# Where the gelu of the dense experts lives: an SBUF tile or the matmul's own PSUM bank

## The chip, the cores and the metric

One core of one Trainium2 chip runs the kernel. The metric is the device time of one execution in microseconds, the median of several runs. The engines are PE (TensorE matmul; PEld its weight loads), DVE (VectorE), ACT (ScalarE), POOL (GpSimd) and SP (SyncE, which here only issues DMAs). Each works through a queue of its own in order; semaphores tie the queues together.

## The reference, cut to what matters

One step of a one-layer hybrid decoder for 1024 prompt tokens and 32 sample rows: adaptive norm, input projection, dilated attention and a delta-rule mixer side by side, output projection, second norm, and a layer of product-key experts. The change touches only the last:

```python
eid  = jnp.take_along_axis(cid, pos, axis=-1)        # 8 heads x 16 experts of 16384 for every token
gate = jax.nn.softmax(top_s, axis=-1)
act  = jax.nn.gelu(jnp.einsum('nd,nhkd->nhk', hb, expert_u[eid]), approximate=False)
return jnp.einsum('nhk,nhkd->nd', gate * act, expert_v[eid])
```

Every expert is one unit: a row of `expert_u` (1024 values) makes a dot with the token, its gelu is multiplied with the gate, and the product scales a row of `expert_v`.

## The kernel before, in words

The kernel computes the experts in two ways at once. Tiles 5, 6 and 7 of the prompt and the sample rows gather the chosen rows by indirect DMA (issued on POOL) and work on DVE: `row<-row,gh` is the product with the token and its sum, `gh<-row,co,gh` or `ga<-row,co,ga` adds a scaled row of `expert_v` to a sum held in PSUM. Tiles 0 to 4 (640 tokens, `n`) are computed densely by `dense` (line 1615): all 16384 units for every token, with a gate of zero where an expert was not chosen.

In `dense`, 128 blocks `b` of 128 units are taken in 32 groups of four (`NG`). `hidden(b)` loads the block's part of `expert_u`, transposed, in two pieces `u`, and splits each into two float32r parts: `uh` by an ACT cast, `ul` by a subtraction on POOL (`split2`, line 1611). For each half `h` of the tokens (320 columns) PE adds 24 matmuls (8 blocks of channels times three products of parts, `mm3`) into one bank of the PSUM tag `d`, which has four banks (`open_psum(ctx, "densep", d=4)`). Then ACT takes the gelu out of the bank into an SBUF tile `act` (two buffers), DVE multiplies it in place with the gates `g`, ACT casts the product to `ch`, and DVE subtracts to get `cl` (`split`, line 230). `values` loads and splits rows of `expert_v` into `vh` and `vl` (POOL, for some blocks DVE). `output` adds 12 matmuls of `ch`, `cl` against `vh`, `vl` into a bank of the same four, and DVE adds the bank to `dacc` in SBUF. A group is thus eight hidden half-tiles and ten output tiles on PE, all of them taking banks of the tag `d`.

The streams are put side by side by `weave`, with a rough meter of engine time, from `run(weave((routed(p_at, [6, 7, NT], "right"), True), fill=[some, all_experts]))` on: the routing of the gathered tiles, the gathers and the dense experts share all queues, and the rest of the dense work runs beside the remaining gathers to the end. The order in each engine's queue is then set by a planner that runs a timeline with costs of its own while the program is built (`schedule_with_timeline_sim=True`); it also adds the semaphore waits, and a bank is given to the next tile once the last instruction that reads it is done. Every instruction is recorded under line 196, the helper that passes calls on, so the trace is read by tiles.

Of the kernel before, what the change touches and what calls it, by code (L numbers as in the profile page):

```python
# [64 lines left out]
def _shape_constants():  # L65
# [20 lines left out]
    # relative bias along distance, from 1023 down  # L86
# [7 lines left out]
    # the sample rows' keys: 4 of every 16 far rows, the near ones, the new ones  # L94
# [35 lines left out]
class _Meter:  # L130
    """a rough count of the engines' time, by which streams of work are put side by side."""
# [43 lines left out]
class _Ring(dict):  # L175
    """tiles by number, made when first asked for."""
# [25 lines left out]
def tile_hybrid_step(ctx, tc, ins, outs):  # L202
# [9 lines left out]
    def open_psum(es, name, side="left", **tags):  # L212
        """banks of PSUM by tag; returns what gives the next one of a tag."""
        pool = es.enter_context(tc.tile_pool(name=name, bufs=1, space=bass.MemoryType.PSUM, side=side, reuse_waits="tile"))

        def bank(tag, n=512):
            return pool.tile([128, n], FT, tag=tag, name=tag, bufs=tags[tag])

        return bank
# [10 lines left out]
    def split(src, hi, lo, eng=None):  # L230
        """src as a sum of two float32r parts."""
        sc.copy(hi, src)
        (eng or ve).tensor_tensor(lo, src, hi.bitcast(FT), op=OP.subtract)

    def piece(pool, src, kn, eng, bufs, wbufs):
        """1024 columns of weights, of kn blocks of rows: as two float32r parts."""
        w = pool.tile([128, 1024], FT, tag="w", name="w", bufs=wbufs).rearrange("p (k c) -> p k c", k=kn)
        sy.dma_start(w, src)
        hl = [pool.tile([128, 1024], FR, tag=f"w{x}", name=f"w{x}", bufs=bufs).rearrange("p (k c) -> p k c", k=kn) for x in "hl"]
        split(w, *hl, eng=eng)  # L240
        return hl

    def mm3(out, l, r, first, last):
        """a product of split operands, to float32's accuracy; or of unsplit ones."""
        if len(l) == 1:
            te.matmul(out, l[0], r[0], start=first, stop=last)
            return
        te.matmul(out, l[0], r[0], start=first, stop=False)
        te.matmul(out, l[0], r[1], start=False, stop=False)
        te.matmul(out, l[1], r[0], start=False, stop=last)  # L250
# [3 lines left out]
    def rsqrt(pool, x, scale, bias, shape, name, floor=None):  # L254
        """1 / sqrt(scale * x + bias), with one Newton step behind the table."""
        n = shape[0]
        t = [pool.tile([128] + list(shape[1:]), FT, tag=f"{name}{j}", name=f"{name}{j}", bufs=2)[:n] for j in range(3)]
        v, y, z = t
        if floor is None:
            ve.tensor_scalar(v, x, scale, bias, op0=OP.mult, op1=OP.add)  # L260
        else:
            ve.tensor_scalar(v, x, floor, None, op0=OP.max)
        sc.activation(y, v, AF.Sqrt)
        ve.reciprocal(y, y)
        ve.tensor_tensor(z, y, y, op=OP.mult)
        ve.scalar_tensor_tensor(z, v, -0.5, z, op0=OP.mult, op1=OP.mult)
        ve.scalar_tensor_tensor(y, z, 1.5, y, op0=OP.add, op1=OP.mult)
        return y
# [7 lines left out]
    def weave(*streams, fill=(), ahead=AHEAD):  # L276
        """several streams side by side: (steps, whether a step waits for the one before). The one that is ready
        first by the meter goes on; fill: streams that only go along."""
# [34 lines left out]
    def open_picked(es, name, tiles, ring=None):  # L313
        """the chosen experts of some tiles, and their gates."""
# [12 lines left out]
    def mod_rows(pool, seg, i, tag, n, bufs=1):  # L327
        """one of the six modulation vectors, a row for every token of tile i."""
# [16 lines left out]
    # ---------------------------------------------------------------- modulation, first norm  # L345
# [7 lines left out]
    def ada_rows(pa, pp, scT, r, bufs):  # L353
# [17 lines left out]
        if r == 2:  # L371
            # the second norm's weights times its scale
            n2 = pa.tile([128, 512], FT, tag="adab", name="n2", bufs=2)
            for g in range(2):
                sy.dma_start(n2[32 * g:32 * g + 32, :], _ap(A["norm2_g"], 512 * g, [[0, 32], [1, 512]]))
            ve.scalar_tensor_tensor(md[:64], md[:64], 1.0, n2[:64], op0=OP.add, op1=OP.mult)
# [17 lines left out]
    def scaled(out, pt, k, ab=ab1):  # L394
        """shift and scale of a norm, of the prompt's transposed rows; k: the block of channels."""
        sc.activation(out, pt, AF.Identity, scale=ab[:, 0, k, 0:1], bias=ab[:, 1, k, 0:1])

    def scaled_sample(out, pt, ab):
        """the same of the sample rows."""
# [4 lines left out]
    def norm_rows(pa, tiles):  # L404
        """the rows of some tiles over their root mean square."""
# [16 lines left out]
    def norm_in(pa, pp, tiles, put):  # L422
        """first norm of some tiles, transposed: put(k, part) for the channels 128 k.. ."""
# [22 lines left out]
    # ---------------------------------------------------------------- projections  # L446
    def project(pw, pp, hT, tiles, bufs=3, wbufs=2, rbufs=1, engs=(gp,)):
        """all columns of w_in for some token tiles: (tile, its column)."""
# [74 lines left out]
    # ---------------------------------------------------------------- the delta-rule heads  # L523
# [11 lines left out]
    def delta_consts(rc):  # L535
# [5 lines left out]
        # tiles that keep zeros where a block is empty  # L541
# [16 lines left out]
    def log_decay(pool, pp, lt, c0, n):  # L558
        """token-major logarithm of the decay."""
# [7 lines left out]
    def key_norms(pool, pp, sqk, n, nj):  # L567
        """1 / max(|kk|, 1e-12), token-major."""
# [8 lines left out]
    def spread(pool, pp, rn, p, n, nj):  # L577
        """the norms of a pair of heads over their columns, transposed."""
# [9 lines left out]
    def group_norm(pool, pp, y, n, bv, g, c0):  # L588
        """y token-major; normalised per head, the bonus and the gate put on, into columns c0.. of the mix."""
# [24 lines left out]
    def rwkv_prompt(pp, side, qs):  # L614
        """quarters of the prompt, 256 tokens each, in chunks of 64; heads go in two groups of four, side by side."""
        n = 256
        both = (0, 1)
        for qi in qs:
            t0 = 256 * qi
            with ExitStack() as es:  # L620
# [3 lines left out]
                with ExitStack() as e2:  # L624
                    pt_ = open_pool(e2, "rwt", side)

                    def shifted(c0, k, tag="shx", out=None):
                        """channels c0.., mixed with the token before."""
# [89 lines left out]
                with ExitStack() as e3:  # L718
# [14 lines left out]
                    # inverses of the 32-blocks: two partitions a block, for its even and its odd rows  # L733
# [30 lines left out]
                def chunk(j, gq, ych, py):  # L764
                    """two chunks of 64 tokens, four heads."""
# [41 lines left out]
                    # right-hand sides [A | M_ak V], then (I - M_ab)^-1 of them  # L807
# [88 lines left out]
    # ---------------------------------------------------------------- dilated attention  # L896
    def attn_bias(pa, pp):
        """the queries' scale by head halves; the relative bias along distance, and of the last 128 queries."""
# [29 lines left out]
    def attn_prompt(pp, side, tiles, nb=None, pa=None, wide=False):  # L928
        """some query tiles of the prompt."""
# [102 lines left out]
    def attn_sample(pp, side, pa=None):  # L1032
        """the sample rows: partition = (row, head, position), four rows at a time."""
        with ExitStack() as es:
# [20 lines left out]
            # masked queries: columns (p, b, h, s)  # L1055
# [103 lines left out]
    def rwkv_sample(pp, side):  # L1159
        n = NS  # L1160
        with ExitStack() as es:
# [11 lines left out]
            # every channel mixed with the token before  # L1173
# [53 lines left out]
            # one partition a (row, head, half of the values)  # L1227
# [38 lines left out]
    # ---------------------------------------------------------------- output projection, second norm  # L1266
    def weights(pa, src, bufs=NW):
        """256 columns of weights in pieces of two blocks of rows; src(first block)."""
# [6 lines left out]
    def shared_banks(pp, tiles):  # L1275
        """256 columns of PSUM for every tile, two tiles in a bank; and whether a tile is its bank's first."""
# [3 lines left out]
    def project_out(pa, pp, tiles, new_x1, new_h2, bufs=NW):  # L1280
        """x1 and the second-norm rows of some tiles; new_x1, new_h2: where they go, the latter transposed."""
# [72 lines left out]
    # ---------------------------------------------------------------- product keys  # L1354
    def fold_keys(pa, pp, bufs):
        """the query projection times the sub-keys."""
# [15 lines left out]
    def route_scores(pa, pp, h2, tops, bufs=NW):  # L1372
        """every half key's scores, for the tiles in h2; the sixteen best of each. The sample rows: a quarter of the
        partitions for every fourth head."""
# [32 lines left out]
    def open_tops(es, name, tiles, side="left", ring=None):  # L1407
        """what route_scores leaves for route_pick."""
# [8 lines left out]
    def route_pick(pick, tops, i, eng=ve):  # L1417
        """the sixteen best experts of every head of a tile's tokens, and their softmax."""
# [38 lines left out]
        for h in range(nh + 1):  # L1457
            if h < nh:
                # the candidate whose place is asked for leaves its expert, the others more (those before it by wrapping)
# [15 lines left out]
    # ---------------------------------------------------------------- experts, gathered  # L1475
# [6 lines left out]
    def expert_dots(gat, pg, eid, gate, h2, npick):  # L1482
        """gate * gelu(u . h2), partition = token."""
# [30 lines left out]
    def sum_rows(gat, acc, co, eid, npick):  # L1514
        """acc = sum of co * v, partition = token."""
# [15 lines left out]
    def gather_sample(gat, pg, acc_bank):  # L1531
        """the sample rows, with a quarter of their experts on each quarter of the partitions."""
# [16 lines left out]
    # ---------------------------------------------------------------- experts, all of them  # L1549
# [3 lines left out]
    def spread_gates(pa, pp, i, c0, iota128, stages):  # L1553
        """the gates of a tile's tokens over all experts: g_d[., second key, first key, token]."""
# [28 lines left out]
        for t4 in range(32):  # L1583
            ps = pp("sp")
            sh = [128, 2, 128]
            for x in range(2):
# [5 lines left out]
                for j in range(2):  # L1592
                    t = slice(o + j, o + j + 1)
                    e = SPREAD[2 * x + j]
                    if e == "sc":
                        # gate * max(1 - |key - column|, 0)
# [18 lines left out]
    def dense(pa, pp, acc, h2T, tiles):  # L1615
        """every expert for the tokens of some tiles: products of split operands."""
# [6 lines left out]
        def hidden(b):  # L1623
# [9 lines left out]
            for h in range(2):  # L1633
# [7 lines left out]
                t = pa.tile([128, n // 2], FT, tag="act", name="act", bufs=2)  # L1641
                sc.activation(t, ps[:, :n // 2], AF.Gelu)
# [54 lines left out]
    # ---------------------------------------------------------------- the order of the work  # L1697
# [192 lines left out]
    def routed(pp, tiles, side):  # L1890
        """from the mix to the experts, for some gathered tiles."""
# [107 lines left out]
```

## Time and profile before

| what | value |
|---|---|
| median of 3 runs | 3811.39 us (3810.4 to 3816.43) |
| profiled execution, span | 3802.4 us |
| PE busy | 3473.4 us (91%) |
| DVE busy | 2899.8 us (76%) |
| POOL busy | 2107.3 us (55%) |
| ACT busy | 1428.1 us (38%) |
| mean DMA rate | 258 GB/s |

The page gives the profiled execution's time as its span, from the first to the last instruction; no other time of that execution is shown. Busy time says how long an engine had an instruction in it; matmuls are pipelined, and a busy PE is not PE at its peak. Rows name what is written and what is read, as `act<-act,g`, with buffer numbers left out, and "idle before" or "waits" tell which instruction's end released a waiting one.

### The profile page before, as it was taken

The numbers are of one execution on the slowest core, as the hardware profiler recorded it, in microseconds if no ns is written. First come the engines' busy times: TensorE is split into PE (matmuls) and PEld (weight loads), VectorE is DVE, ScalarE is ACT, GpSimd is POOL, SyncE is SP. The second block draws the span as 40 slices with busy tenths as digits, with TensorE's granted clock in tenths as the row PEclk, the third lists the DMA queues.
The fourth block names the chain that finished last, engine by engine and source line by source line (L and its number), as shares of the span: only waits on it lengthen the run. The fifth ranks groups of instructions, "written<-read, shape, count | busy, mean of one in ns | idle before, by whom it ended". The sixth has DMA issues, their size and how long they took to land.

```text
span 3802.4 us, 57197 instructions
## 1 busy us (share of the span) xinstructions
PE 3473.4 (91%) x19618; PEld 2873.5 (76%) x19618; DVE 2899.8 (76%) x6059; ACT 1428.1 (38%) x3124; POOL 2107.3 (55%) x1842
## 2 busy tenths in 40 slices
PE   7999999789889888969999989999999999999998
PEld 3878678567768664547877879888887878788886
DVE  2655364588688566777878999888888888888898
ACT  5544344336766654542411322222222222222221
POOL 3232021015555356656655777677677767677775
PEclk8999999899999899989999999999999999999999
DMA  9643695553765667749988779999889898899998
GB/s 292 196 143 115 189 280 170 164 181 134 241 210 179 206 222 229 259 156 328 324 303 283 230 263 327 320 317 312 308 303 318 306 315 303 307 312 320 327 324 311
DMA packets 592528, 981.58 MB, mean 258 GB/s; under 512 B 78323, under 2 KB 354620, under 8 KB 589420
## 3 DMA queue, kind: packets, MB, share of 16 engines
q1 hardware_dynamic: 467788, 524.84, 43.1%
q0 software_dynamic: 124448, 453.08, 33.9%
q8 instruction: 155, 2.54, 0.3%
q14 instruction: 137, 1.12, 0.1%
HBM read 882.97 MB, written 94.78 MB: 257 GB/s over the span
## 4 chain that ended last, share of the span: by engine, by line
PE 36%; DVE 23%; DMA 19%; issue 11%; POOL 8%; ACT 3%; SPq 1%; POOLq 0%; DVEq 0%; ACTq 0%
PE at L196 10%; PE d L196 9%; DMA u<-in_uT 8%; PE rw L196 5%; PE pj L196 5%; POOL row L196 4%; PE rs L196 3%; DVE gh L196 3%; DVE act L196 2%; DVE row L196 2%; DVE cl L196 2%; PE sp L196 2%; DMA row<-in_expert_v,eid 2%; POOL vl L196 2%; POOL ul L196 2%
## 5 line engine op out<-in xcount | busy, mean ns | idle before, releaser
L196 PE MATMUL d<-h2T,uh 128*128 128x320 f32 x4096 | 908.1, 311 | 11.6 <-ACT h2T L196 7.0
L196 PEld LDWEIGHTS d<-h2T,uh 128*128 128x128 f32 x4096 | 689.7, 189 | 21.2 <-ACT h2T L196 7.3
L196 PE MATMUL d<-h2T,ul 128*128 128x320 f32 x2048 | 632.8, 310 | 0.3 <-POOL ul L196 0.3
L196 POOL DMA_INDIRECT row<-in_expert_u,eid x416 | 405.7, 975 | 264.3 <-DVE co L196 90.0
L196 PE MATMUL d<-vl,ch 128*128 128x512 f32 x1280 | 512.2, 401 | 43.6 <-POOL vl L196 43.6
L196 PE MATMUL d<-vh,ch 128*128 128x512 f32 x1280 | 486.4, 401 | 51.2 <-DVE dacc L196 26.9
L196 DVE CUSTOM_DVE_ANT_0 row<-row,gh 128x1024 f32<-128x1024 f32 x416 | 499.4, 1210 | 34.7 <-DMA row<-in_expert_u,eid 26.0
L196 POOL DMA_INDIRECT row<-in_expert_v,eid x416 | 406.4, 977 | 183.5 <-DVE gh L196 66.2
L196 PE MATMUL d<-vh,cl 128*128 128x512 f32 x1280 | 505.6, 396 | 0.8 <-DVE cl L196 0.7
L196 POOL TENSOR_SCALAR oha<-c_iota,tr 128x128 f32<-128x128 f32 x320 | 309.6, 974 | 310.8 <-PE sp L196 297.9
L196 POOL TENSOR_TENSOR ul<-u,uh 128x512 fp32r<-128x512 f32 x256 | 336.6, 1324 | 139.7 <-ACT uh L196 129.7
L196 ACT CAST vh<-v 128x512 fp32r<-128x512 f32 x256 | 157.5, 620 | 623.2 <-DMA v<-in_expert_v 447.9
L196 PEld LDWEIGHTS d<-h2T,ul 128*128 128x128 f32 x2048 | 386.2, 189 | 2.7 <-issue 1.6
L196 DVE SCALAR_TENSOR_TENSOR gh<-row,co,gh 128x1024 f32<-128x1024 f32 x285 | 364.9, 1280 | 27.7 <-DMA row<-in_expert_v,eid 26.0
L196 PEld LDWEIGHTS d<-vh,ch 128*128 128x128 f32 x1280 | 243.0, 191 | 129.8 <-DVE dacc L196 43.3
L196 DVE TENSOR_TENSOR act<-act,g 128x320 f32<-128x320 f32 x256 | 279.2, 1090 | 77.2 <-ACT act L196 72.8
L196 POOL TENSOR_TENSOR wl<-w,wh 128x1024 fp32r<-128x1024 f32 x50 | 122.5, 2453 | 388.7 <-ACT wh L196 353.9
L196 PEld LDWEIGHTS d<-vl,ch 128*128 128x128 f32 x1280 | 244.4, 191 | 112.0 <-POOL vl L196 62.1
L196 POOL TENSOR_TENSOR vl<-v,vh 128x512 fp32r<-128x512 f32 x224 | 289.5, 1301 | 34.7 <-ACT vh L196 30.3
L196 ACT CAST ch<-act 128x320 fp32r<-128x320 f32 x256 | 117.7, 460 | 495.4 <-DVE act L196 464.2
L196 PEld LDWEIGHTS d<-vh,cl 128*128 128x128 f32 x1280 | 244.9, 191 | 53.9 <-DVE cl L196 2.0
L196 ACT CAST uh<-u 128x512 fp32r<-128x512 f32 x256 | 154.0, 617 | 257.0 <-DMA u<-in_uT 166.2
(449 smaller groups left out, 6932.7 us busy)
## 6 DMA issues: line engine op xcount, KB each, us to landing
u<-in_uT SPq DMA_DIRECT2D x256, 256.0 KB
v<-in_expert_v SPq DMA_DIRECT2D x256, 256.0 KB
w<-wq_d SPq DMA_DIRECT2D x224, 256.0 KB
g_d<-stage SPq DMA_DIRECT2D x20, 2048.0 KB
g<-g_d SPq DMA_DIRECT2D x64, 640.0 KB
w<-in_w_in SPq DMA_DIRECT2D x75, 512.0 KB
w<-in_w_out SPq DMA_DIRECT2D x112, 256.0 KB
adaw<-in_ada_w SPq DMA_DIRECT2D x32, 512.0 KB
```

Of the source, the lines that this page charges most:

```text
L196: return f(*a, **k)
```

## The change

The SBUF tile `act` for a half-tile of hidden units is gone. `t` is now the used part of the PSUM bank itself: the gelu writes back to where it reads, the product with the gates is made in the bank, and the cast to `ch` and the subtraction for `cl` read the bank. The pool's tag `act` stays for `gate2` at the end of `dense`. The rest of the diff takes out comments and leaves their lines empty, so line numbers stay except one.

```diff
@@ -1638,8 +1638,9 @@
                 ps = pp("d")
                 for k in range(KD):
                     mm3(ps[:, :n // 2], (uh[:, k], ul[:, k]), [x[:, k, cs] for x in h2T], k == 0, k == KD - 1)
-                t = pa.tile([128, n // 2], FT, tag="act", name="act", bufs=2)
-                sc.activation(t, ps[:, :n // 2], AF.Gelu)
+
+                t = ps[:, :n // 2]
+                sc.activation(t, t, AF.Gelu)
                 tv = t.rearrange("p (s t) -> p s t", t=32)
                 ve.tensor_tensor(tv, tv, G_[h][:, :, b % 4], op=OP.mult)
                 split(t, ch[:, cs], cl[:, cs])
```

## Rows read from the trace of the kernel before

**Rows 1.** The page: span, and busy time with share and instructions of each engine.
```profile
span 3802.4 us, 57197 instructions
PE 3473.4 (91%) x19618; PEld 2873.5 (76%) x19618; DVE 2899.8 (76%) x6059; ACT 1428.1 (38%) x3124; POOL 2107.3 (55%) x1842
```

**Rows 2.** Table of stretches: length, busy time of each engine, granted clock, DMA share, GB/s.
```profile
1718.00:3802.00 2084.00, 1969.69 (x10564) 1707.73 (x10562) 1793.72 (x2702) 535.07 (x1074) 1458.16 (x1325) 0.99 0.89 307
...
2080.00:2240.00 160.00, 144.61 (x781) 127.37 (x780) 157.00 (x364) 47.31 (x86) 120.96 (x101) 0.98 0.72 238
...
2900.00:3490.00 590.00, 549.87 (x2989) 487.83 (x2988) 506.26 (x630) 149.99 (x309) 424.42 (x389) 0.99 0.90 310
```

**Rows 3.** Instruction groups of DVE, 1718 to 3802 us: busy, mean ns, idle before.
```profile
L196 DVE TENSOR_TENSOR act<-act,g 128x320 f32<-128x320 f32 x256 | 279.2, 1090 | 77.2 <-ACT act L196 72.8 <-issue 2.8 <-ACT vh L196 0.9
L196 DVE TENSOR_TENSOR cl<-act,ch 128x320 fp32r<-128x320 f32 x256 | 215.0, 840 | 45.6 <-ACT ch L196 39.9 <-issue 4.7 <-ACT vh L196 0.8
```

**Rows 4.** The tile `act`: min/median/max duration in ns, first and last start.
```profile
L196 ACT ACTIVATE act<-d x256: 421/432/442, 1718.1 to 3756.5; 128x320 f32<-128x320 f32 x128
L196 DVE TENSOR_TENSOR act<-act,g x256: 433/534/5453, 1718.5 to 3758.8; 128x320 f32<-128x320 f32 x128
L196 ACT CAST ch<-act x256: 440/460/468, 1719.3 to 3759.3; 128x320 fp32r<-128x320 f32 x128
L196 DVE TENSOR_TENSOR cl<-act,ch x256: 465/491/4156, 1720.7 to 3760.4; 128x320 fp32r<-128x320 f32 x128
```

**Rows 5.** The same view of the tiles `dacc`, `vl` and `row`.
```profile
L196 DVE TENSOR_TENSOR dacc<-dacc,d x310: 661/676/690, 1860.2 to 3789.2; 128x512 f32<-128x512 f32 x155
...
L196 DVE TENSOR_TENSOR vl<-v,vh x32: 676/692/2478, 1715.3 to 3689.9; 128x512 fp32r<-128x512 f32 x32
...
L196 DVE CUSTOM_DVE_ANT_0 row<-row,gh x416: 1189/1208/1225, 1733.3 to 3495.7; 128x1024 f32<-128x1024 f32 x139
```

**Rows 6.** Timeline, 3015.8 to 3017.6 us: start, duration, engine, instruction.
```profile
3015.87 1.31 POOL L196 TENSOR_TENSOR vl<-v,vh 128x512 fp32r<-128x512 f32 x1
3016.15 1.38 DVE L196 TENSOR_TENSOR cl<-act,ch 128x320 fp32r<-128x320 f32 x1
```

**Rows 7.** The chain of waits that ended last, 1718 to 3802 us, by line.
```profile
by line: issue 16.3%; PE d L196 15.8%; DMA u<-in_uT 13.4%; POOL row L196 7.6%; PE at L196 5.9%; DVE gh L196 4.8%; DVE act L196 4.4%; DVE cl L196 4.1%; DVE row L196 4.0%; DMA row<-in_expert_v,eid 3.5%; POOL vl L196 3.3%; POOL ul L196 2.9%; D
```

**Rows 8.** PE's waits, 1700 to 3802 us: us in total, times, longest.
```profile
PE d L196 <- POOL vl L196: 43.6, 39, 4.8
PE d L196 <- DVE dacc L196: 26.9, 35, 2.1
```

**Rows 9.** Timeline of PE, ACT and DVE at the first and last late subtraction.
```profile
2108.28 0.46 PE L196 MATMUL d<-h2T,uh 128*128 128x320 f32 x2
...
2108.72 0.46 PE L196 MATMUL d<-h2T,uh 128*128 128x320 f32 x2
...
2111.56 0.48 DVE L196 TENSOR_TENSOR cl<-act,ch 128x320 fp32r<-128x320 f32 x1
...
3654.40 0.62 ACT L196 CAST uh<-u 128x512 fp32r<-128x512 f32 x1 [2.96 <-DMA u<-in_uT]
...
3656.84 0.39 PE L196 MATMUL d<-vh,ch 128*128 128x512 f32 x1
...
3657.52 0.39 PE L196 MATMUL d<-vh,ch 128*128 128x512 f32 x1
...
3657.85 0.48 DVE L196 TENSOR_TENSOR cl<-act,ch 128x320 fp32r<-128x320 f32 x1
```

**Rows 10.** Instruction groups of DVE, 2080 to 2240 us.
```profile
L196 DVE TENSOR_TENSOR act<-act,g 128x320 f32<-128x320 f32 x18 | 24.9, 1382 | 0.1
...
L196 DVE TENSOR_TENSOR cl<-act,ch 128x320 fp32r<-128x320 f32 x18 | 14.6, 814 | 0.0
```

**Rows 11.** Waits of ACT and of SP's DMA queue in the dense stage.
```profile
ACT act L196 <- DVE cl L196: 16.3, 6, 7.6
...
SPq L196 <- DVE act L196: 186.5, 54, 10.1
```

## The prediction

> **What bounds the kernel now.** I read the page's share of busy time first [rows 1]: PE is busy 91% of the span and DVE 76%. An average over stages with different limits says little, so the second view is the table by stage [rows 2]. The dense experts run from 1718 us to the end, 2084 us, with PE busy 1969.7 us: 114 us are all that anything in this stage can give back without taking work from PE. DVE is busy 1793.7 us, 86%, and the DMA engines 89%. In one stretch, 2080 to 2240 us, DVE is busy 157 of 160 us and sets the pace alone.
>
> The third view is what DVE does there [rows 3]: the product with the gates takes 1090 ns on average and the subtraction that makes the low part 840 ns, for 320 columns. The fourth is the spread of these durations [rows 4]: medians of 534 and 491 ns with tails to 5453 and 4156 ns, so the means are made by a few long ones. The fifth shows which forms have such a tail [rows 5]: the accumulation of the outputs, with one operand in a PSUM bank, stays between 661 and 690 ns over 310 executions, and the gathered rows' product (its second operand is a bank) between 1189 and 1225 over 416. The DVE subtraction for `vl`, with both operands in SBUF, has a minimum of 676 ns and a maximum of 2478. The sixth shows one long one at work [rows 6]: `cl` starts 0.28 us behind a GpSimd product that reads SBUF and takes 1.38 us; it ends 0.35 us after that product does. So the tail is DVE held up by GpSimd, and only the forms with two SBUF operands are hit.
>
> The seventh view is the chain of waits [rows 7]: over the dense stage DVE's `act` has 4.4% of it and `cl` 4.1%, 177 us together. The last is PE's own waits [rows 8]: 43.6 us for GpSimd's `vl`, 26.9 us for a bank that DVE's accumulation has yet to read.
>
> **DVE's two products.** After the change the gate product reads the bank and the gates, the subtraction the bank and `ch`: one SBUF operand each, which is the kind without a tail in [rows 5]. The trace has no such product that writes into a bank with 320 columns. Bounds: the accumulation's 676 ns scaled by 320/512, 0.42 us, below; those 676 ns unscaled, though for 512 columns, above. I take 0.50, nearest to the undisturbed executions in [rows 4]. Now the two cost 279.2 + 215.0 = 494.2 us [rows 3]; then 512 x 0.50 = 256. DVE is freed of 238 us (148 to 279 by the bounds; a loss is excluded, since even 676 ns is below both means).
>
> [...]
>
> **What of it lies on the path.** In 2080 to 2240 us, where DVE is full, the 18 + 18 instructions take 24.9 + 14.6 us [rows 10] and would take 18: 21 us come off whole. Over the whole stage 238/494 = 48% of the 177 us in the chain is 85 us; less those 21, 64 us lie where DVE is not full and PE or the DMA queues are close behind. Of these I take half, 32, halfway between all hidden and none hidden. Gain 53 us, with bounds 0 and 85. What is late next is PE itself, then the loads of `u` and `v`.
>
> **The bank is held longer.** Now a hidden unit's bank is free after the gelu; then only after gelu, product, cast and subtraction. There are four banks, in order, so PE's first matmul of the fourth tile on waits for the subtraction, on PE's queue with every later matmul behind it, the routing's too. I went through all 256 hidden half-tiles (24 matmuls each; an output tile has 12, and a group is 8 of the first and 10 of the second) and set the end of `cl` against the start of the fourth tile on. The median end is 3.0 us before it. In 53 cases it is behind, the first and the last in [rows 9]: `cl` ends at 2112.0 where PE has gone on at 2108.3, and at 3658.3 where PE has gone on at 3656.8. The last shows why: ACT, in order, waits 2.96 us for the load of `u` before the gelu behind that cast has its turn. Neighbours share a wait, so a run counts by its worst: two runs in DVE's full stretch (8.8 and 10.5 us) and 45 us in the other 38 cases, 64 us. With each case's own product and subtraction cut to 0.5 us, 35 us are left. A wait here is partly taken back: PE arrives later at the next output tiles, where it now waits for `vl` or for a bank [rows 8]. I take 20 us, a little over half, with bounds 0 and 64.
>
> **Edits at nothing.** ACT's gelu writes to a bank and its cast reads one: 432 ns from a bank against 460 from SBUF [rows 4] is 256 x 28 ns = 7 us of ACT work either way, and ACT is busy 535 of 2084 us [rows 2]; if that cover were gone it would cost or give 7 us. The two SBUF tiles `act` go as a limit: ACT now waits 16.3 us in 6 places for the subtraction before the next gelu [rows 11]; I count it as nothing, since the four banks put a limit in its place. The loads of the gates wait on SP for the product that read the old ones, 186.5 us in 54 places [rows 11], with the loads of `u` and `v` behind them; an earlier product lets them go earlier, and that is in the chain's 85 us.
>
> **Sum.** 3802.4 - 53 + 20 = 3769 us of span. The page gives the profiled execution by its span alone; the median of the runs is 3811.4, 9.0 us more, which I put down to what lies around the span. So 3778 us, 33 less than before (0.9%).
>
> **Rivals.** A measurement of this kernel can tell 0.2%, 7.6 us, from no change.
> - The bank is the new wait (slower). Place: PE's first matmul of the fourth tile after a hidden one, behind `cl` on DVE. Price: the full 64 us, nothing taken back, against half of the 85: 3811 + 64 - 43 = 3832 us. It decides where bank-holding exceeds the 8.2 to 10.6 us that the three tiles between take (36 matmuls at 0.227 us or 72 at 0.147 us, by the starts in [rows 9]), and then only if the holding doesn't shrink with DVE's load. For it: 53 cases already, and gelu and cast stand in ACT's in-order queue behind casts that wait for loads. Against it: the median has 3 us to spare and the tails in the chain are what goes. [...]
> - All hidden (same): the freed DVE time becomes DVE idle time, because PE at 94.5% and the DMA engines at 0.89 set the pace, and what the full stretch gives goes into the bank's waits: 3811 - 21 + 20 = 3810 us. For it: both shares are high everywhere [rows 2]. Against it: PE's two largest waits end at GpSimd and DVE, not at a load [rows 8].
> - Everything comes through (much faster): 85 us, no bank wait: 3726 us. It needs most of PE's 114 idle us to go.
> - The change doesn't do what it says: the products keep their tails, because the gates and `ch` are still in SBUF, and the bank's half price of 20 us is left: 3831 us. Against it: no form with one bank operand shows a tail [rows 5].
>
> The order of each engine's queue is written out by a planner with costs of its own, and it may come out otherwise; no row prices that, and it is why the range is wider than the sum's.
>
> **Chances.** Forecast 0.50 (own range 3735 to 3800), bank 0.22, hidden 0.15, everything 0.10, no effect on the tails 0.03. Faster by over 0.2%: 0.50 + 0.10 = 0.60. Same: 0.15. Slower: 0.22 + 0.03 = 0.25. The range of 3725 to 3835 leaves out the lower half of the fourth case and the upper half of the bank's, some 0.16.
>
> **What would show it.** Right: the gate product and the subtraction at 0.45 to 0.55 us each with no execution over 0.7; DVE busy in the dense stage near 1555 us; PE's waits for `vl` and for the accumulation smaller; new waits of PE for `cl` of some 20 us. Wrong: means over 0.7 us for the two; PE waiting over 50 us for `cl`; PE's busy time falling below 94% of the stage; or the two products short and PE's idle time as before, which would be the third case.

## The result, and the profile after

The kernel after takes 3765.4 us in the median of four runs, against 3813.9 us before; the ratio is 0.9873 (95% interval 0.9846 to 0.9900). The forecast was 3778 us. The profiled execution has a span of 3751.3 us, 51.1 us less than before.

The page, span and busy time; the rows of before are [rows 1]:

```profile
span 3751.3 us, 57270 instructions
PE 3453.9 (92%) x19618; PEld 2873.9 (77%) x19618; DVE 2693.2 (72%) x6059; ACT 1431.2 (38%) x3122; POOL 2080.6 (55%) x1842
```

DVE has the same 6059 instructions and 206.6 us less busy time. The table of stretches (length; busy time of PE, PEld, DVE, ACT and POOL; granted clock, DMA share, GB/s), against [rows 2]:

```profile
1718.00:3751.00 2033.00, 1949.56 (x10547) 1709.39 (x10546) 1592.91 (x2701) 535.37 (x1069) 1430.57 (x1325) 0.99 0.91 315
...
2080.00:2240.00 160.00, 138.88 (x742) 124.50 (x741) 153.28 (x367) 40.61 (x77) 119.55 (x105) 0.96 0.78 253
...
2900.00:3490.00 590.00, 564.30 (x3105) 507.23 (x3104) 451.87 (x643) 159.81 (x321) 433.98 (x405) 0.99 0.93 323
```

and between the last two, before and then after:

```profile
2240.00:2900.00 660.00, 626.09 (x3399) 554.85 (x3398) 564.12 (x740) 174.95 (x355) 479.09 (x437) 0.98 0.91 313
```
```profile
2240.00:2900.00 660.00, 639.50 (x3548) 575.55 (x3547) 516.21 (x793) 188.10 (x376) 495.25 (x459) 0.99 0.94 326
```

The dense stage is 51 us shorter, PE is busy for 95.9% of it in place of 94.5%, and the DMA engines move 315 GB/s in place of 307. Of the 51 us, 31 are PE's idle time (114 us before, 83 after) and 20 are PE's busy time, for nearly the same matmuls; since their ends are modelled, the trace does not say why. Where the gain fell can be read from PE's instructions in equal stretches of time: 39 fewer in 2080 to 2240 us, where DVE is full, then 149 more and 116 more in the two stretches behind it. The durations of the two operations and of the two around them, in the view of the tile (min/median/max in ns), against [rows 4]:

```profile
L196 ACT ACTIVATE d<-d x256: 387/423/437, 1716.5 to 3712.7; 128x320 f32<-128x320 f32 x128
L196 DVE TENSOR_TENSOR d<-d,g x256: 475/498/508, 1716.9 to 3715.2; 128x320 f32<-128x320 f32 x128
L196 ACT CAST ch<-d x256: 398/427/436, 1717.7 to 3715.7; 128x320 fp32r<-128x320 f32 x128
L196 DVE TENSOR_TENSOR cl<-d,ch x256: 470/486/506, 1718.2 to 3717.2; 128x320 fp32r<-128x320 f32 x128
```

No product takes over 508 ns where the longest took 5453. The counterpart of [rows 6], in the timeline after:

```profile
3358.88 2.56 POOL L196 TENSOR_TENSOR vl<-v,vh 128x512 fp32r<-128x512 f32 x2
...
3359.23 0.49 DVE L196 TENSOR_TENSOR cl<-d,ch 128x320 fp32r<-128x320 f32 x1
```

`cl` starts 0.35 us behind GpSimd's subtraction (0.28 there) and is done in 0.49 us while GpSimd goes on. Over the whole of both traces it is the same: before, all 115 products and 75 subtractions that took over 0.7 us overlapped a GpSimd operation on SBUF tiles (`ul`, `vl` or `tq`) and ended 0.34 to 0.36 us after one had ended; after, 219 of the 512 start while such an operation runs, and none is longer than the 508 ns. As groups (busy, mean ns, idle before them), against [rows 3]:

```profile
L196 DVE TENSOR_TENSOR d<-d,g 128x320 f32<-128x320 f32 x256 | 126.8, 496 | 155.6 <-ACT d L196 142.4 <-DMA g<-g_d 12.7
L196 DVE TENSOR_TENSOR cl<-d,ch 128x320 fp32r<-128x320 f32 x256 | 124.4, 487 | 33.6 <-ACT ch L196 33.5
L196 DVE TENSOR_TENSOR vl<-v,vh 128x512 fp32r<-128x512 f32 x32 | 47.2, 1476 | 24.9 <-ACT vh L196 21.9 <-issue 2.8
```

The product now sits behind an idle DVE, waiting for the gelu (142.4 us in place of 72.8). The chain that ended last, over the dense stage, against [rows 7]:

```profile
by line: PE d L196 41.6%; issue 9.6%; DMA u<-in_uT 9.0%; PE at L196 6.5%; POOL row L196 5.5%; DMA row<-in_expert_v,eid 5.4%; POOL vl L196 3.4%; DVE gh L196 3.1%; DMA v<-in_expert_v 2.3%; POOL ul L196 1.8%; DMA row<-in_expert_u,eid 1.8%; DMA
```

The 8.5% of product and subtraction have left the head of the list; PE's dense matmuls have 41.6% in place of 15.8%. PE's own waits (us in total, times, longest) after, against [rows 8]:

```profile
PE d L196 <- POOL vl L196: 42.9, 31, 2.9
PE d L196 <- DVE cl L196: 18.8, 5, 5.7
PE d L196 <- ACT h2T L196: 7.9, 1, 7.9
PE d L196 <- DVE dacc L196: 6.2, 9, 1.3
```

and the further ones of before that are no longer there:

```profile
PE d L196 <- ACT act L196: 10.5, 8, 3.3
PE d L196 <- ACT ch L196: 8.6, 6, 2.3
```

The wait for a bank that the accumulation has yet to read fell by 20.7 us, those for gelu and cast by 19.1; the new wait for the subtraction is 18.8 us, and the wait for `vl` did not move.

### The profile page after: what moved, and what is told of

It reads as the page before. It is cut to its first block, busy times and chain, and to the rows that moved or that the text cites. A ratio compares the mean times of both kernels' runs of the same rounds, so it can differ in the third digit from the quotient of the medians.

```text
span 3751.3 us, 57270 instructions
## 1 busy us (share of the span) xinstructions
PE 3453.9 (92%) x19618; PEld 2873.9 (77%) x19618; DVE 2693.2 (72%) x6059; ACT 1431.2 (38%) x3122; POOL 2080.6 (55%) x1842
## 4 chain that ended last, share of the span: by engine, by line
PE 51%; DMA 18%; DVE 14%; issue 7%; POOL 6%; ACT 3%; SPq 1%; POOLq 0%; DVEq 0%; ACTq 0%
PE d L196 23%; PE at L196 10%; PE rw L196 5%; PE pj L196 5%; DMA u<-in_uT 5%; PE rs L196 3%; POOL row L196 3%; DMA row<-in_expert_v,eid 3%; PE sp L196 2%; POOL vl L196 2%; DVE gh L196 2%; DVE ohb L196 1%; DMA v<-in_expert_v 1%; DMA w<-wq_d 1%; POOL ul L196 1%
## 5 line engine op out<-in xcount | busy, mean ns | idle before, releaser
L196 PE MATMUL d<-vl,ch 128*128 128x512 f32 x1280 | 508.3, 398 | 42.9 <-POOL vl L196 42.9
L196 POOL DMA_INDIRECT row<-in_expert_u,eid x416 | 394.7, 949 | 242.0 <-DVE co L196 89.6
L196 PE MATMUL d<-vh,ch 128*128 128x512 f32 x1280 | 478.3, 396 | 17.2 <-DVE cl L196 9.7
L196 POOL DMA_INDIRECT row<-in_expert_v,eid x416 | 397.1, 955 | 166.2 <-issue 46.2
L196 DVE TENSOR_TENSOR dacc<-dacc,d 128x512 f32<-128x512 f32 x310 | 206.2, 683 | 47.8 <-PE d L196 47.6
L196 DVE TENSOR_TENSOR d<-d,g 128x320 f32<-128x320 f32 x256 | 126.8, 496 | 155.6 <-ACT d L196 142.4
```

The costliest lines, as they stand in the source:

```text
L196: return f(*a, **k)
```

## The experiments

Two theories. **Tails:** a DVE operation with two SBUF operands is held up by a GpSimd operation on SBUF tiles (means of 1090 and 840 ns [rows 3]), the change took that away, and the freed DVE time is the gain, less a price for the longer hold of the banks. **Order:** the trace can't show whether the gain came from the planner's other order of the queues and from the limit of two `act` tiles, both of which changed too. The runs were taken in three groups, each on one chip with the kernel before beside it: e7_still, e2_prod, e3_sub and e1_act3v; then e9_after, e8_both, e10_after_order and e11_before_order; then the other four. Ratios are to the kernel before in the same group, whose medians were 3808.3, 3807.7 and 3811.8 us. The unchanged kernel after ran in the second group (0.9869), so a difference to it from another group is one of two ratios. The diffs are shortened to what matters.

**One operand back to SBUF, nothing else moved.** The gate product reads a part of `h2T`; every queue's order is that of the kernel after. The gelu's value is left out of the product.

```diff
-ve.tensor_tensor(tv, tv, G_[h][:, :, b % 4], op=OP.mult)
+still = h2T[0][:, 0, cs].bitcast(FT)        # same shape as t, viewed as tv
+ve.tensor_tensor(tv, still, G_[h][:, :, b % 4], op=OP.mult)
```

> The kernel after, but the gate product takes its first operand from a part of h2T in SBUF in place of the bank (so the gelu's value is left out of the result); it still writes the bank, waits for the gelu, and every queue has the instructions of the kernel after in the same order. Theory tails (a DVE instruction with two SBUF operands is held up by GpSimd's reads, and that is what the change took away): the product's mean goes back from 0.496 us to about 1.0 to 1.1 with single ones over 2 us, the subtraction stays at 0.487, DVE gets 130 to 160 us busier, and 157/250 of the gain goes: 3785 to 3805 us. Rival order (the gain is from another order of the queues and from the limit of two act tiles that went): 3765 us, within 8.

Measured 3777.9 us, ratio 0.9927 (0.9906 to 0.9947). The product in the view of its tile, and the two operations as groups:

```profile
L196 DVE TENSOR_TENSOR d<-h2T,g x256: 474/778/3523, 1716.4 to 3740.9; 128x320 f32<-128x320 f32 x128
```
```profile
L196 DVE TENSOR_TENSOR d<-h2T,g 128x320 f32<-128x320 f32 x256 | 268.2, 1048 | 119.0 <-ACT d L196 105.9 <-DMA g<-g_d 12.7
...
L196 DVE TENSOR_TENSOR cl<-d,ch 128x320 fp32r<-128x320 f32 x256 | 123.2, 482 | 34.7 <-ACT ch L196 34.5
```

One operand's memory makes the tail: at the same order the mean goes from 0.496 to 1.048 us and the maximum from 508 to 3523 ns, while the subtraction beside it stays short. The time follows: against the kernel after (0.9869) it is 0.0058 of 3808, 22 us, which the two intervals leave between 10 and 34. That is at the low end of the 20 to 40 us that I expected, and 3777.9 us itself lies under the 3785 to 3805.

**The two halves.** The product reads the bank and writes an SBUF tile; or the gelu goes to SBUF and the product writes the bank.

```diff
 p = ps[:, :n // 2]                                    # e2_prod: cast and subtraction read t in SBUF
+sc.activation(p, p, AF.Gelu);  ve.tensor_tensor(t, p, gates, op=OP.mult);  split(t, ...)
 p = ps[:, :n // 2]                                    # e3_sub: cast and subtraction read the bank
+sc.activation(t, p, AF.Gelu);  ve.tensor_tensor(p, t, gates, op=OP.mult);  split(p, ...)
```

> Half of the change: the gelu stays in the bank, the gate product reads it there and writes an SBUF tile; cast and subtraction read SBUF. Theory tails: product near 0.5 us, subtraction keeps a mean near 0.85; about 60% of the gain, and the bank is free after the product, so nearly no waits of PE for it: 3770 to 3790 us. Rival order: two act tiles are a limit as before, so 3814 us, within 10.

Measured 3773.8 us, ratio 0.9904 (0.9880 to 0.9928): product 0.483 us, subtraction 0.898.

> The other half: the gelu goes to an SBUF tile, the gate product reads it there and writes the bank, cast and subtraction read the bank. Theory tails: product keeps a mean near 1.1 us, subtraction near 0.49; 35 to 40% of the gain and the whole cost of the bank's longer hold: 3790 to 3815 us. Rival order: a new order of the queues as in the kernel after, near 3765 us.

Measured 3796.5 us, ratio 0.9970 (0.9952 to 0.9988): product 1.083 us, subtraction 0.481. Each half behaves as the operands say. e3_sub has the same tails and about the same hold of the bank as e7_still and is 0.0043 slower, some 16 us; its order differs and its gelu writes one of two `act` tiles. Which of the two causes it was not told apart.

**The limit of two tiles alone.** Three `act` tiles in the kernel before.

```diff
-t = pa.tile([128, n // 2], FT, tag="act", name="act", bufs=2)
+t = pa.tile([128, n // 2], FT, tag="actt", name="act", bufs=3)
-gate2[dh] = pa.tile([128, 512], FT, tag="act", name="g2", bufs=2)
+gate2[dh] = pa.tile([128, 512], FT, tag="v", name="g2", bufs=2)
```

> The kernel before with three tiles act in place of two (the last gates of the residual move to the tag v for room). No operand changes its memory. Theory tails: product and subtraction keep their means of 1.09 and 0.84 us, and the time stays at 3814 us, within 8. Rival order: the limit on the gelu goes and the planner writes another order, so a good part of the 49 us comes: 3770 to 3795 us.

Measured 3811.8 us, ratio 1.0012 (0.9995 to 1.0028); the means stay at 1.070 and 0.843 us. The limit was worth nothing that shows, and the order that the planner made of it neither.

**The kernel after again, and both kernels in another order.**

```diff
-AHEAD = 3000
+AHEAD = 2000
```

> The kernel after again, unchanged, so that the others of this call have it on the same chip. Both theories: a ratio of 0.985 to 0.990 to the kernel before, 3755 to 3775 us.

Measured 3757.8 us, ratio 0.9869 (0.9845 to 0.9894).

> The kernel after with the same instructions in another order: the priority that the planner gives to the streams in front is 2000 in place of 3000. It shows how much an order alone is worth. Theory tails: it keeps most of its lead on the kernel before, 3755 to 3785 us. Rival order: the lead belonged to one order, and this one is near 3800 us or above.

Measured 3757.8 us, ratio 0.9858 (0.9832 to 0.9885).

> The kernel before with the same instructions in another order, by the same priority of 2000. Theory tails: within 15 us of the kernel before, and 30 to 60 us above the kernel after in that order. Rival order: it can come out anywhere, 3770 us included.

Measured 3815.3 us, ratio 1.0022 (1.0006 to 1.0039). The lead of the kernel after is 1.3% in the one order and 1.6% in the other; this other order moved neither kernel by more than some 8 us. The gain is there in both orders.

**Both tails back, the hold kept.** The subtraction takes one scalar of each row from the bank, so the bank is not free earlier; gelu and product are left out of what it computes.

```diff
+still = h2T[0][:, 0, cs].bitcast(FT)        # viewed as sv for the product
+ve.tensor_tensor(tv, sv, G_[h][:, :, b % 4], op=OP.mult)
+sc.copy(ch[:, cs], t)
+ve.scalar_tensor_tensor(cl[:, cs], still, t[:, 0:1], ch[:, cs].bitcast(FT), op0=OP.mult, op1=OP.subtract)
```

> The kernel after with both DVE operations given two SBUF operands again (a part of h2T stands in for the bank's values, which leaves the gelu out of the product and the product out of the low part); the subtraction takes one scalar of each row from the bank, so the bank is held just as long as after. The planner writes another order. Theory tails: all of the relief is gone and only the longer hold is left: means near 1.05 and 0.85 us, PE waits of 30 to 60 us for cl, and 3815 to 3840 us, slower than the kernel before. Rival order: the limit of two act tiles is still gone and the queues are as free as after: 3765 to 3790 us.

Measured 3818.0 us, ratio 1.0019 (1.0004 to 1.0034). Its two groups and PE's waits:

```profile
L196 DVE TENSOR_TENSOR d<-h2T,g 128x320 f32<-128x320 f32 x256 | 262.7, 1027 | 57.3 <-ACT d L196 52.8 <-DMA g<-g_d 4.0
L196 DVE SCALAR_TENSOR_TENSOR cl<-h2T,d,ch 128x320 fp32r<-128x320 f32 x256 | 232.8, 910 | 37.9 <-ACT ch L196 37.8
```
```profile
PE d L196 <- POOL vl L196: 56.8, 37, 4.0
PE d L196 <- DVE cl L196: 37.0, 24, 7.4
PE d L196 <- DVE dacc L196: 11.5, 11, 3.2
```

With the tails back all of the gain is gone: 1.0019 - 0.9869 = 0.0150, 57 us, is what the two tails cost in this form of the kernel, the longer hold that they bring included: from the last matmul to the end of the subtraction the median is 6.9 us here and 3.6 in the kernel after. That longer hold, without relief, is 0.0019 above before, 7 us (1.5 to 13 by the interval). The planner's order differs here too, and an order could be as much as 8 us, so the 7 is a size and not a proof.

**One bank fewer.**

```diff
-pd = open_psum(ctx, "densep", d=4)
+pd = open_psum(ctx, "densep", d=3)
```

> The kernel after with three banks for the dense experts in place of four, so the bank that a subtraction frees is wanted one tile (2.7 to 3.5 us) earlier. In the trace after, the median time from a hidden tile's last matmul to the end of its subtraction is 3.6 us and the 95th percentile 9.7, against two tiles of 5.4 to 7 us. Theory tails: the bank is a price of its own that shows as soon as a bank is missing: PE waits for cl of 40 to 80 us in place of 19, 3780 to 3810 us. Rival (a bank costs nothing, the hold is short enough): 3758 us, within 10.

Measured 3807.1 us, ratio 1.0000 (0.9984 to 1.0017). PE's waits:

```profile
PE d L196 <- POOL vl L196: 50.8, 31, 4.0
PE d L196 <- DVE cl L196: 26.1, 12, 12.2
PE d L196 <- DVE dacc L196: 23.6, 8, 10.5
```

A missing bank costs 0.0131, 50 us, as much as the change brings. That is more than the waits that are booked to banks grew, 7.3 us for `cl` and 17.4 for the accumulation, so part of it shows elsewhere; the wait for `cl` stayed under the 40 us that I expected. The kernel before with three banks was not run, so how much of the 50 us is due to the longer hold, and how much any kernel with three banks would pay, was not told apart.

**What PE waits for next: `vl`.** More of it on DVE, or more tiles for the loads, in the room of the two `act` tiles.

```diff
-POOL_LO = (1, 2, 3, 4, 5, 6, 7, 8, 9)
+POOL_LO = (1, 2, 3, 5, 6, 7, 8, 9)                    # e6_vl
-v  bufs=2, gate2 in tag "act"
+v  bufs=4, gate2 in tag "v"                           # e12_v4
-u  bufs=3, v bufs=2, gate2 in tag "act"
+u  bufs=4, v bufs=3, gate2 in tag "v"                 # e13_u4v3
```

> The kernel after with the subtraction for vl on DVE for two of eight blocks in place of one (32 instructions more on DVE, 32 less on POOL). PE's largest wait after is 43 us for vl on POOL. Theory tails: DVE has time to spare but vl has two SBUF operands there, near 1.4 us each, so the new instructions bring a tail back: within 12 us of the kernel after. Rival (POOL's load is what PE waits for): the wait for vl falls to 25 us and the time to 3735 to 3750 us.

Measured 3750.8 us, ratio 0.9847 (0.9817 to 0.9877), which can't be told from the kernel after; `vl` on DVE takes 1.438 us each, and PE's wait for POOL's `vl` is 47.0 us, so the rival's 25 did not come.

> The kernel after with the room of the two act tiles given to the loads of expert_v: four tiles v in place of two (the residual's gates move to that tag). ACT waits 452 us for v after, and POOL's vl stands behind it. If the depth of the loads sets PE's wait for vl: the wait falls to 20 to 30 us, 3735 to 3750 us. If POOL's own load sets it: 3758 us, within 8.

Measured 3727.3 us, ratio 0.9789 (0.9763 to 0.9815), faster than either side expected.

> The same room given to one more tile u (four) and one more tile v (three). If the depth of the loads is the limit: 3735 to 3750 us, with ACT's wait for u below 150 us. If not: 3758 us, within 8.

Measured 3706.7 us, ratio 0.9732 (0.9703 to 0.9760), the fastest of all, and far under the 3735 that I expected at best. PE's waits in e12_v4 and then in e13_u4v3:

```profile
PE d L196 <- DVE cl L196: 15.9, 7, 5.8
PE d L196 <- POOL vl L196: 12.6, 7, 5.2
...
PE d L196 <- DVE dacc L196: 7.0, 4, 3.5
```
```profile
PE d L196 <- DVE dacc L196: 10.9, 6, 3.3
...
PE d L196 <- DVE cl L196: 5.3, 1, 5.3
PE d L196 <- POOL vl L196: 1.4, 1, 1.4
```

and ACT's waits for the loads in the kernel after and then in e13_u4v3:

```profile
ACT vh L196 <- DMA v<-in_expert_v: 451.9, 119, 10.9
...
ACT uh L196 <- DMA u<-in_uT: 212.2, 67, 10.5
```
```profile
ACT vh L196 <- DMA v<-in_expert_v: 171.4, 58, 7.3
ACT uh L196 <- DMA u<-in_uT: 28.5, 8, 6.8
```

The wait for `vl` goes with the depth of the loads in front of DVE and POOL and not with the work of either (47.0 us in e6_vl, with 32 subtractions moved to DVE): two more tiles take it from 42.9 us to 1.4, and take 0.0137, 52 us, off the time, as much again as the change did. The order differs in these runs too, but the other order above was worth some 8 us at most.

## Why the prediction was right, point by point

- **The operands.** "I take 0.50" for each product: measured 0.496 and 0.487 us, none over 0.508. DVE was freed of 494.2 - 251.2 = 243 us in the two groups (238 forecast). e7_still shows the cause with nothing else moved, and the timelines before and after show GpSimd as the one that holds the operation up (its operation in [rows 6] is a subtraction, not a product). With both inputs in SBUF the product took up to 3523 ns in e7_still, with one in the bank 508 at most. That it is GpSimd's reads, as the expectation of e7_still has it, no run shows: its `ul`, `vl` and `tq` read SBUF tiles and write them. The forecast took no price for a bank as a source, and none shows in the subtraction: its median is 486 ns from the bank and was 491 from SBUF [rows 4].
- **DVE's busy time** in the stage fell by 201 us to 1593, not to the forecast 1555. The two groups gave their 243; other DVE operations took some back: `vl` on DVE, which still has two SBUF operands, went from 0.935 to 1.476 us each, 17 us, and the routing's `td` and `tc` from 10.7 to 20.0 us together. Of the 32 `vl` on DVE, 25 overlap a GpSimd operation on SBUF tiles, where 9 did before; the others take 0.69 us in both.
- **What lies on the path.** Forecast 53 us, measured 57 between e8_both and e9_after, but the place was wrong, and that the two sizes agree has luck in it. In 2080 to 2240 us 21 us were to come off whole. The product and the subtraction do take 16.5 us there in place of 39.5 [rows 10], yet DVE stays full (153 of 160 us) and PE gets 39 instructions fewer done. Some of DVE's groups there, with forms taken together, before and then after:

```profile
L196 DVE SCALAR_TENSOR_TENSOR gh<-row,co,gh 128x1024 f32<-128x1024 f32 x47 | 60.0, 1276 | 0.1
...
L196 DVE TENSOR_TENSOR td<-tf 128x64 f32<-128x64 f32 (+10 forms) x21 | 4.7, 285 | 0.0
```
```profile
L196 DVE SCALAR_TENSOR_TENSOR gh<-row,co,gh 128x1024 f32<-128x1024 f32 x56 | 71.9, 1284 | 4.1 <-DMA row<-in_expert_v,eid 3.7
...
L196 DVE TENSOR_TENSOR td<-tf 128x64 f32<-128x64 f32 (+10 forms) x21 | 11.2, 591 | 0.0
L196 DVE TENSOR_TENSOR d<-d,g 128x320 f32<-128x320 f32 x17 | 8.3, 493 | 1.1 <-ACT d L196 1.1
L196 DVE TENSOR_TENSOR cl<-d,ch 128x320 fp32r<-128x320 f32 x17 | 8.2, 486 | 0.0
```

  Nine more accumulations of gathered rows (12 us) and longer routing operations filled the freed time. The gain came behind it, where only half of the chain's 64 us was to come through, a half that no row supported. By halves: the product's tail alone costs 22 us (e7_still) or 38 (e3_sub), the subtraction's alone 13 (e2_prod, with a shorter hold), sums of 35 and 51 against 57 for both. With intervals of some 12 us on each, these runs do not show whether the halves add up.
- **The bank.** Forecast 20 us; e8_both gives 7 for the hold, and that is some 13 of the 15 us by which the forecast fell short (33 us forecast, 48 measured). The wait for `cl` did appear, 18.8 us in 5 places, and I had said some 20. What I missed is that the hold shrinks with the tails: over all 256 half-tiles the median from the last matmul to the end of the subtraction went from 7.0 to 3.6 us, the gelu's own wait from 1.9 to 0.5. The cases that were behind by a little went away, and 14.8 of the 18.8 us left lie in three places in DVE's full stretch. This is the bank rival's own condition ("if the holding doesn't shrink with DVE's load"), and it decided against that rival; and even where the holding did not shrink, in e8_both, it cost 7 us and not 64. e4_after3 shows that banks are short, with three of them the time is that of the kernel before, but not that the longer hold is the reason.
- **The waits for `vl`** were to get smaller with DVE's relief. They did not (43.6 to 42.9 us). What fell are the waits for the accumulation, the gelu and the cast; e12_v4 and e13_u4v3 (12.6 and 1.4 us) show that `vl` waited for loads.
- **9.0 us around the span** was a wrong reading: the profiled run after took 3753.1 us with a span of 3751.3, so 1.8 us lie around it, and the rest of the 9.0 was the difference between one execution and the median. After the change that whole gap is 14.1 us (3765.4 - 3751.3).
- **The other rivals.** All hidden and no effect on the tails are out by the ratio and by the durations. Everything through (3726 us) was not reached: PE still waits for `vl` and `cl` (42.9 and 18.8 us).

## What to carry to other kernels

Before moving an elementwise chain, compare minimum, median and maximum of each form: here a long tail on the DVE operations with two SBUF operands (to 5453 ns for a median of 534), and none on those with one in PSUM (661 to 690 ns for the accumulation), pointed to GpSimd. The timeline settled it: every product and subtraction over 0.7 us ended 0.34 to 0.36 us after a GpSimd operation did, and reading one operand from the matmul's bank removed the tail (508 ns at most). A bank held through the chain is weighed by the chain's length against the time of the tiles in between, here 3.6 us in the median against 8.2 to 10.6 us for three tiles, so count the banks first (with three in place of four the kernel took 50 us longer), and count the chain with the tails gone (7.0 us with them). The gain need not come where the freed engine is fullest: here the gathers took 12 us of the room in 2080 to 2240 us. Then look at PE's waits again: here the SBUF that the change left unused was worth 52 us, as much as the change itself, as depth for the loads.

## What the runs showed that I had not expected

Taking 243 us of DVE time away was worth 50 us of the kernel's, and none of that shows in the stretch where DVE is fullest. And a form that keeps two SBUF operands is not steady: `vl` on DVE took 0.935 us each before, 1.476 after, 1.729 in e12_v4 and 0.850 in e13_u4v3, though nothing in it changed. It goes with how many of the 32 overlap a GpSimd operation on SBUF tiles, 9, 25, 27 and 5; those that overlap none take 0.69 us on average in each of the four runs.
